# Rounding and subtracting a decoder step's weights 1024 columns at a time, in six tiles of their own

## The chip, the cores and the metric

The kernel runs on one core of one Trainium2 chip. The metric is the device time of one execution in microseconds (us). The core has five instruction streams that run side by side and wait for each other through semaphores: PE (matmuls, with their weight loads shown as PEld), ACT, DVE, POOL, and SP, which here issues all transfers between the chip's memory and the core's on-chip buffers.

## What is computed

One inference step of a one-layer hybrid decoder for 512 prompt tokens and 8 x 8 sample tokens, 576 columns in all, with a model width of 1024. Cut to what matters:

```python
mod = silu(c) @ w_ada + b_ada                 # six shifts and gains
u = x * (1 + sc1) + sh1
qa, ka, va, qh, fh, ih, ogh, gate_a, gate_b = split(u @ w_in)
attn = merge(dilated_attention(g) for g in ((128, 1), (512, 4), (2048, 16)))
hg = rms_norm(hgrn2(silu(qh), f, ih)) * silu(ogh)
merged = sigmoid(gate_a) * (attn @ w_branch_a) + sigmoid(gate_b) * (hg @ w_branch_b)
x1 = layer_norm(ALPHA * x + g1 * (merged @ w_out))
u2 = x1 * (1 + sc2) + sh2
x2 = layer_norm(ALPHA * x1 + g2 * (relu(u2 @ w_up + b_up) ** 2 @ w_down + b_down))
```

All arrays are fp32. Besides x2 the kernel returns the new key/value caches and the new HGRN2 states.

## The kernel before

**Products in three terms.** Every large product is made from rounded parts. A value w is split into `hi` (w rounded to the fp32r type, by an ACT copy) and `lo` (w minus hi, rounded, by a DVE subtraction). PE then adds three products: hi times hi, hi times lo and lo times hi. The activations are split the same way (`uh`/`ul`, `u2h`/`u2l`, `hdh`/`hdl` and so on).

**Weights.** `unit(...)` lists the weight blocks in the order of use. A unit is 8 (branch a: 4) k tiles of 128 rows by W columns, W being 256 or 512. `load_one` brings 8 KB a partition at a time into one of three `raw` buffers (`NRAW`), so a unit of 256 columns is one load, a unit of 512 columns two. A block of 128 columns is split by `split_slot`: for each four k tiles one ACT copy and one DVE subtraction of 4 x 128 = 512 columns, into two pages. Token units (`tok=True`: the v of the three attention groups and the two HGRN value units, with the tokens as the matmul's stationary operand) are split by `split_k`, one k tile of 512 columns at a time: four k tiles ahead of the first half of the unit, four ahead of the second (`split`, `j // 5 * 4`).

**Pages.** Nearly all tiles on the chip come from one pool, `pages`: `NPG` = 68 buffers of 2304 bytes a partition (576 fp32 columns). Activations, heads, scores, cache tiles (`kv`), broadcast queries (`qb`), states and the split weights share it. A tile gets a buffer when its first writer is put in order, and that writer waits until the last instruction that uses the buffer's former tile is done. Each engine runs its instructions strictly in the order in which the program lists them.

**The front and the back.** The front runs from the input to the branch products: all units up to `n_front`. Its first unit (`u0`, 512 columns, two loads) is special: three of its blocks (`n_early`) are split slot by slot and multiplied k tile by k tile (`early_mm`) as the input's k tiles `uh`/`ul` come into being (`make_u`), slot 0 before the first, slot 1 at the end of step s = 1. Then a loop goes over the blocks (`flat`): `ahead(i)` and `ahead(i + 1)` split the next block, `run_block` lists the matmuls of the current one and the evacuation of its result. The back (w_out, layer norm, the MLP's 32 up and 32 down blocks) follows after `side.drain()`.

**The order of the work.** Attention, the sample caches, HGRN and the ada products are generators in lanes of `Side`. After each group of up to 8 matmuls `side.pump` lets the lanes emit steps, by a planned clock of every engine (`Engine`: ACT 90 + 0.84 n, DVE 65 + 1.05 n, POOL 60 + 2.28 n ns for n columns). So the planned costs set where side steps fall among the matmuls.

Nearly every instruction is recorded through one helper, so the profile gives them all one line, L173; they are told apart by their tiles: `whi`/`wlo` the split weights, `wraw` a raw buffer, `lin` the result bank of the large products.

Of the kernel before, what the change touches and what calls it, by code (L numbers as in the profile page):

```python
# [12 lines left out]
F32R = mybir.dt.float32r  # L13
U8 = mybir.dt.uint8
AF = mybir.ActivationFunctionType
# [4 lines left out]
KT = D // 128  # L20
# [5 lines left out]
HF = NT // 2  # L26
# [22 lines left out]
LND = 1200  # L49
APART = 6  # L50
LNQ = 3200
NPG = 68
AHEAD_K = 8
LN2 = 2500
SPH = 0
NRAW = 3
# [187 lines left out]
def decoder_step(ctx, tc, I, O):  # L244
    nc = tc.nc
    consts = ctx.enter_context(tc.tile_pool(name="consts", bufs=1))
    pages = ctx.enter_context(tc.tile_pool(name="pages", bufs=NPG))
    raw = ctx.enter_context(tc.tile_pool(name="raw", bufs=NRAW))
    small = ctx.enter_context(tc.tile_pool(name="small", bufs=2))
    dram = ctx.enter_context(tc.tile_pool(name="dram", bufs=1, space=bass.MemoryType.DRAM))  # L250
    psum = ctx.enter_context(tc.tile_pool(name="psum", bufs=2, space=bass.MemoryType.PSUM))
# [2 lines left out]
    V, A = Engine(nc.vector, "DVE", 65.0, 1.05), Engine(nc.scalar, "ACT", 90.0, 0.84)  # L254
    G, PE, SP = Engine(nc.gpsimd, "POOL", 60.0, 2.28), Engine(nc.tensor, "PE", 0.0, 0.0), Engine(nc.sync, "SP", 0.0, 0.0)
# [5 lines left out]

    def page(shape, name, dtype=F32):
        return pages.tile(shape, dtype, name=name, tag="page")

    def bank(shape, tag, bufs=2):
        return psum.tile(shape, F32, name=tag, tag=tag, bufs=bufs)
# [30 lines left out]
    units = []  # L297

    def unit(src, row0, nk, col0, W, blocks, tok=False):
        units.append(dict(src=src, row0=row0, nk=nk, col0=col0, W=W, blocks=blocks, slots=[], w={}, tok=tok))  # L300
# [19 lines left out]
    def load_more(force=False):  # L320

        while leaving and (force or leaving[0] <= side.now):
            leaving.popleft()
        while load_q and live[0] + len(leaving) < NRAW:
            load_one()
# [3 lines left out]
    def loaded(u):  # L329
        return sum(kk for _, kk, _ in u["slots"]) == u["nk"]  # L330

    def weights_done(slots):
        live[0] -= len(slots)
        leaving.extend(Engine.read.get(t.tensor.name, 0.0) for _, _, t in slots)
        load_more()

    def split(u, j):


        def there():  # L340
            load_more(True)
            return len(u["slots"]) > j // 5 if u["tok"] else loaded(u)
        if not there():
            side.drain(("a", "s"), there)
        assert there()
        if u["tok"]:
            for k in range(j // 5 * 4, j // 5 * 4 + 4):
                split_k(u, k)
            return
        for s in range(len(u["slots"])):  # L350
            split_slot(u, j, s)
        if j == len(u["blocks"]) - 1:
            weights_done(u["slots"])

    def split_k(u, k, eng=V):

        if k in u["w"]:
            return
        load_more(True)
        t = u["slots"][k // 4][2][:, k % 4]  # L360
        w = u["w"][k] = page([128, 512], "whi", F32R), page([128, 512], "wlo", F32R)
        A.activation(w[0], t, AF.Copy)
        eng.tensor_sub(w[1], t, w[0])
        if k % 4 == 3:
            weights_done(u["slots"][k // 4:k // 4 + 1])

    def split_once(u, j):
# [1 line left out]
            u["split"].add(j)  # L369
            split(u, j)  # L370

    def split_slot(u, j, s):
        k0, kk, t = u["slots"][s]
        hi, lo = u["w"].setdefault(j, ([], []))
        for k in range(0, kk, 4):
            src = t[:, k:k + 4, j * 128:(j + 1) * 128]
            hi.append(page([128, 4, 128], "whi", F32R))
            lo.append(page([128, 4, 128], "wlo", F32R))
            A.activation(hi[-1], src, AF.Copy)
            V.tensor_sub(lo[-1], src, hi[-1])  # L380

    def mm_part(w, nk, xs, h, ps, ks):
        hi, lo = w
        seq = [(hi, 0), (hi, 1), (lo, 0)]
        n = 0
        for k in ks:
            for m, (ww, xi) in enumerate(seq):
                PE.matmul(ps, ww[k // 4][:, k % 4], xs[xi][k][:, h * HF:(h + 1) * HF],
                          start=(k == 0 and m == 0), stop=(k == nk - 1 and m == 2))
                n += 1  # L390
                if n % 8 == 0 and n < 3 * len(ks):
                    side.pump(8 * 123.0)
# [68 lines left out]
    def hv(t, h):  # L461
        return t[:, h * HF:(h + 1) * HF]
# [1028 lines left out]
    n_front = len(units)  # L1491
    for n0 in (0, 4):
        unit(I["w_out"][0], 0, 8, n0 * 128, 512, [None] * 4)
    for qd in range(4):
        for n0 in (0, 4):
            unit(I["w_up"][0], 0, 8, (qd * 8 + n0) * 128, 512, [None] * 4)
        for n0 in (0, 4) if qd < 3 else (4, 0, 4):
            unit(I["w_down"][0], qd * 1024, 8, n0 * 128, 512, [None] * 4, tok=(qd == 3))
    for u in units:
        for k0 in range(0, u["nk"], 2048 // u["W"]):  # L1500
            load_q.append((u, k0))
# [58 lines left out]
    xs = [page([128, 4, 128], "xs", F32R) for _ in range(2)]  # L1560
# [13 lines left out]
    u0 = units[0]  # L1574
# [9 lines left out]
    x_transposed(xa, range(4))  # L1584
    for j in range(n_early):
        done_split.add((id(u0), j))
        split_slot(u0, j, 0)
    shift = [ada(s, w) for s, w in enumerate(wa)]
    wa.clear()
    next(shift[0])  # L1590
    for s in range(4):
        next(shift[s])
        for k in (2 * s, 2 * s + 1):
            make_u(k)
        if s == 3:
            ahead(n_early)
        if s:
            early_mm(2 * s - 1)
        if s == 2:
            next(shift[3])  # L1600
        early_mm(2 * s)
        if s < 2:
            next(shift[s + 1])
            x_transposed(xb, (2 * s, 2 * s + 1))
        if s == 1:
            for j in range(n_early):
                split_slot(u0, j, 1)
    early_mm(KT - 1)
    shift.clear()
    for j in range(n_early):  # L1610
# [8 lines left out]
    for i, (u, j) in enumerate(flat):  # L1619
# [18 lines left out]
        if n_run == 20:  # L1638
            for e in range(2):
                t = page([128, 4, 128], "lmf")  # L1640
# [106 lines left out]
    for k in range(KT):  # L1747
        t = page([128, NT], "hT")
# [31 lines left out]
    def half(u, j, xs, h, evac):  # L1780
        ps = bank([128, HF], "lin")
        mm_half(u["w"][j], 8, xs, h, ps)
        evac(h, ps)
        side.pump(8 * 123.0)
# [4 lines left out]
    u = mlp[0]  # L1789
# [75 lines left out]
    ud = mlp[14:17]  # L1865
    for i, (u, j, xs, ev) in enumerate(seq):
        if i < 4:
            for k in (2 * i, 2 * i + 1):
                for h in range(2):
                    G.tensor_mul(hv(hT[k], h), hv(hT[k], h), rstds[h])  # L1870
        if i == n_down:
            side.add("p", residual())
        if i + 1 < len(seq):
            split(*seq[i + 1][:2])
        else:
            for k in range(AHEAD_K):
                split_k(ud[0], k)
        if i >= 8:
            copy_rows()
        for h in range(2):  # L1880
            half(u, j, xs, h, ev)
        u["w"].pop(j)
# [85 lines left out]
    def blocks(w, e):  # L1968
        for n in range(4):
            ps = bank([128, NT - NM], "lin")  # L1970
            for k in range(KT):
                if n == 0 and k + AHEAD_K < KT:
                    split_k(w, k + AHEAD_K)
                for m, (xi, wi) in enumerate(TERMS):
                    PE.matmul(ps, w["w"][k][wi][:, n * 128:(n + 1) * 128], HD[xi][k][:, NM:NT],
                              start=(k == 0 and m == 0), stop=(k == KT - 1 and m == 2))
                if n == 3 and w is ud[0]:
                    pass_on(w, k, ud[1])
                if k % 2 and k < KT - 1:
                    side.pump(6 * 136.0)  # L1980
            gated(hT[4 * e + n], ps, slice(NM, NT), 5, 4 * e + n)
            side.add("pr"[n % 2], tokens_major(4 * e + n))
            side.pump(6 * 136.0)

    def pass_on(u, k, v):

        if k >= 2:
            u["w"].pop(k - 2)
        if k >= KT - AHEAD_K:
            split_k(v, k - KT + AHEAD_K)  # L1990

    def tiles(w, e):
        for c in range(NM // 128):
            last = c == NM // 128 - 1

            def before(k):
                if w is ud[1]:
                    if last and k >= 2:
                        w["w"].pop(k - 2)
                    if k % 2 == SPH:  # L2000
                        split_k(ud[2], 4 * c + k // 2, V if c else G)

            for cols in (slice(0, 256), slice(256, 512)) if e and last else (slice(0, 512),):
                ps = mm_tokens(w["w"], HD, lambda t: t[:, c * 128:c * 128 + 128], range(KT), before, cols,
                               "att" if cols.start else "lin")
                add_up(c, e, ps, cols)
            if e:
                if last:
                    side.drain()
                moments(c, c + 1)  # L2010
                normalize(c, last)
# [43 lines left out]
```

## Time and profile before

| | us |
|---|---|
| median of 3 runs | 1381.82 |
| lowest and highest of the 3 | 1379.16 and 1386.65 |
| the profiled execution | 1381.52 |
| its span in the profile | 1379.7 |

The mean granted clock of the profiled execution was 0.989. Its busy times and the rows behind them are shown where the prediction uses them. In a row of a group, "xN | a, b | c" is the number of instructions, their busy time in us, the mean of one in ns, and the engine's idle time in us just before them with what ended it. In a row of the timeline the first two numbers are the start and the time in us, and the bracket holds the idle time before it with what ended that. In a row of waits stand the us in total, the number of waits and the longest.

### The profile page before, as it was taken

To read this page: it belongs to the slowest core of one execution; us is meant where nothing else is said; L and a number is where in the kernel's file an instruction comes from. 1 tells how busy PE (TensorE), PEld (TensorE's weight loads), DVE (VectorE), ACT (ScalarE), POOL (GpSimd) and SP (SyncE) were. 2 spreads that over 40 slices of the span, in tenths; PEclk is the share of its full clock that TensorE was granted. 3 is DMA by queue.
4 is the path that set the end of the run, shared out by engine and by line. 5 is a ranking of instruction groups with operands and counts; after the bars stand their busy time and mean duration, and the time that the engine had idled before them with its cause. 6 is when DMAs were issued, how large, how long until landed. Compare 5 with 4: busy or idle time off the path is not lost.

```text
span 1379.7 us, 24690 instructions
## 1 busy us (share of the span) xinstructions
PE 1330.6 (96%) x9624; PEld 1228.2 (89%) x9624; DVE 766.6 (56%) x1572; ACT 469.5 (34%) x1101; POOL 359.9 (26%) x419
## 2 busy tenths in 40 slices
PE   6999999999899999999999999999999999999995
PEld 3899898799778887888899999998999999999994
DVE  2456555558767886566655446547522333354458
ACT  3423333332422232333233441325554422413522
POOL 1242023026417563234344200003500200200205
PEclk9999999999999999999999999999999999999998
DMA  9789899689989977776445223331123633522322
GB/s 295 255 306 341 268 317 339 238 272 324 280 282 285 319 243 242 240 239 199 147 157 170 70 73 112 130 123 62 62 107 129 237 124 147 220 77 91 118 99 69
DMA packets 184520, 269.40 MB, mean 195 GB/s; under 512 B 15756, under 2 KB 92372, under 8 KB 183892
## 3 DMA queue, kind: packets, MB, share of 16 engines
q1 hardware_dynamic: 184404, 267.83, 57.7%
q8 instruction: 76, 1.25, 0.4%
q14 instruction: 40, 0.33, 0.1%
HBM read 210.45 MB, written 74.10 MB: 206 GB/s over the span
## 4 chain that ended last, share of the span: by engine, by line
PE 83%; DVE 6%; DMA 4%; ACT 2%; issue 2%; POOL 2%; SPq 1%; DVEq 0%; POOLq 0%; ACTq 0%
PE lin L173 68%; PE att L173 7%; PE tr L173 4%; PE sx L173 4%; DVE wlo L173 2%; DMA out_dram<-kv 2%; DVE res L173 1%; DMA kv<-in_cache_kv_w_dram 1%; POOL qb L173 1%; ACT whi L173 1%; SPq L173 1%; DMA xtm<-in_x_prompt_dram 0%; DMA wraw<-in_w_ada_dram 0%; DMA qb<-qsc 0%; DVE st L173 0%
## 5 line engine op out<-in xcount | busy, mean ns | idle before, releaser
L173 DVE TENSOR_TENSOR wlo<-wraw,whi 128x512 fp32r<-128x512 f32 x340 | 248.4, 774 | 128.5 <-ACT whi L173 125.7
L173 PE MATMUL lin<-uh,whi 128*128 128x288 f32 x992 | 298.4, 301 | 4.3 <-DVE hso L173 2.4
L173 PE MATMUL lin<-uh,wlo 128*128 128x288 f32 x992 | 298.2, 301 | 2.3 <-DVE wlo L173 2.3
L173 PE MATMUL lin<-ul,whi 128*128 128x288 f32 x992 | 299.3, 302 | 1.0 <-DVE ul L173 0.9
L173 ACT ACTIVATE whi<-wraw 128x512 fp32r<-128x512 f32 x344 | 193.4, 620 | 112.8 <-DMA wraw<-in_w_down_dram 29.7
L173 PEld LDWEIGHTS lin<-ul,whi 128*128 128x128 f32 x992 | 187.6, 189 | 13.7 <-issue 10.9
L173 PEld LDWEIGHTS lin<-uh,whi 128*128 128x128 f32 x992 | 187.5, 189 | 10.3 <-DVE hso L173 2.7
L173 PEld LDWEIGHTS lin<-uh,wlo 128*128 128x128 f32 x992 | 187.7, 189 | 7.1 <-issue 3.8
L173 POOL TENSOR_TENSOR qb<-qb,kv 128x512 f32<-128x512 f32 x96 | 128.3, 1356 | 204.0 <-DMA qb<-qsc 90.7
L173 PE MATMUL lin<-u2h,whi 128*128 128x288 f32 x496 | 147.1, 297 | 1.2 <-ACT u2h L173 1.2
L173 PE MATMUL lin<-u2l,whi 128*128 128x288 f32 x496 | 147.0, 296 | 0.3 <-DVE u2l L173 0.3
L173 PE MATMUL lin<-u2h,wlo 128*128 128x288 f32 x496 | 146.8, 296 | 0.0
L173 PE MATMUL lin<-hdh,whi 128*128 128x288 f32 (+1 forms) x448 | 133.6, 298 | 0.2 <-ACT hdh L173 0.2
L173 PE MATMUL lin<-hdl,whi 128*128 128x288 f32 (+1 forms) x448 | 132.9, 297 | 0.1
L173 PE MATMUL lin<-hdh,wlo 128*128 128x288 f32 (+1 forms) x448 | 133.0, 297 | 0.0
L173 POOL TENSOR_TENSOR rel<-rel 128x288 f32<-128x288 f32 x56 | 38.3, 684 | 292.7 <-ACT rel L173 287.7
L173 PEld LDWEIGHTS lin<-u2h,whi 128*128 128x128 f32 x496 | 93.4, 188 | 1.8 <-ACT u2h L173 1.5
L173 PEld LDWEIGHTS lin<-u2l,whi 128*128 128x128 f32 x496 | 93.3, 188 | 1.5 <-DVE u2l L173 0.9
L173 DVE TENSOR_TENSOR hdl<-rel,hdh 128x288 fp32r<-128x288 f32 x61 | 28.4, 466 | 118.5 <-ACT hdh L173 118.5
L173 PEld LDWEIGHTS lin<-u2h,wlo 128*128 128x128 f32 x496 | 93.3, 188 | 0.5 <-issue 0.5
L173 PEld LDWEIGHTS lin<-hdh,whi 128*128 128x128 f32 x448 | 84.1, 188 | 0.7 <-ACT hdh L173 0.4
L173 PEld LDWEIGHTS lin<-hdl,whi 128*128 128x128 f32 x448 | 84.1, 188 | 0.3 <-DVE hdl L173 0.3
(358 smaller groups left out, 2546.6 us busy)
## 6 DMA issues: line engine op xcount, KB each, us to landing
wraw<-in_w_in_dram SPq DMA_DIRECT2D x42, 1024.0 KB
kv<-in_cache_kv_w_dram SPq DMA_DIRECT2D x144, 256.0 KB
qb<-qsc SPq DMA_DIRECT2D x96, 256.0 KB
wraw<-in_w_down_dram SPq DMA_DIRECT2D x18, 1024.0 KB
out_dram<-kv SPq DMA_DIRECT2D x64, 256.0 KB
wraw<-in_w_ada_dram SPq DMA_DIRECT2D x16, 1024.0 KB
wraw<-in_w_up_dram SPq DMA_DIRECT2D x16, 1024.0 KB
out_dram<-in_cache_kv_w_dram SPq DMA_DIRECT2D x32, 512.0 KB
```

The costliest lines, as they stand in the source:

```text
L173: return f(out, *args, **kw)
```

## The change

The front's splits become twice as wide where a raw buffer holds enough, and they move from the pages into a pool of their own: `NWP` = 6 tiles of 8 x 128 fp32 columns (4 KB a partition). The pages are 59 instead of 68, so that 9 x 2304 = 20736 bytes a partition go and 24576 come.

- A block of a 256-column unit is split by one ACT copy and one DVE subtraction of 8 x 128 columns. Blocks of the first unit and of branch a keep 512 columns (a raw buffer holds four of their k tiles) but use the new tiles as well.
- A token unit's k tiles go in pairs of 2 x 512 columns for k = 0 to 5; k = 6 and 7 are split one by one into pages as before.
- The back is split as before (`four`, `two=False`), into pages.
- `AHEAD_K` goes: it was 8, the number of k tiles, so nothing changes by that.

```diff
-NPG = 68
-AHEAD_K = 8
+NPG = 59
+NWP = 6
...
+    parts = ctx.enter_context(tc.tile_pool(name="parts", bufs=NWP))
...
+    def wpart(shape, name, dtype=F32R):
+
+        return parts.tile(shape, dtype, name=name, tag="part")
...
         if u["tok"]:
             for k in range(j // 5 * 4, j // 5 * 4 + 4):
-                split_k(u, k)
+                split_k(u, k, two=(k < 6))
             return
-        for s in range(len(u["slots"])):
-            split_slot(u, j, s)
+        split_block(u, j, four=u.get("four", False))
...
+        k -= k % 2
+        t = u["slots"][k // 4][2][:, k % 4:k % 4 + 2]
+        hi, lo = wpart([128, 2, 512], "whi"), wpart([128, 2, 512], "wlo")
+        A.activation(hi, t, AF.Copy)
+        eng.tensor_sub(lo, t, hi)
+        for i in range(2):
+            u["w"][k + i] = hi[:, i], lo[:, i]
+        if k % 4 == 2:
             weights_done(u["slots"][k // 4:k // 4 + 1])
...
-    def split_slot(u, j, s):
-        k0, kk, t = u["slots"][s]
-        hi, lo = u["w"].setdefault(j, ([], []))
-        for k in range(0, kk, 4):
-            src = t[:, k:k + 4, j * 128:(j + 1) * 128]
-            hi.append(page([128, 4, 128], "whi", F32R))
-            lo.append(page([128, 4, 128], "wlo", F32R))
-            A.activation(hi[-1], src, AF.Copy)
-            V.tensor_sub(lo[-1], src, hi[-1])
+    def split_block(u, j, slots=None, four=False):
+
+        if j not in u["w"]:
+            u["w"][j] = [], []
+        for k0, kk, t in u["slots"] if slots is None else [u["slots"][s] for s in slots]:
+            if four:
+                for k in range(0, kk, 4):
+                    split_rows(u, j, t[:, k:k + 4, j * 128:(j + 1) * 128], page)
+            else:
+                split_rows(u, j, t[:, :, j * 128:(j + 1) * 128], wpart)
+
+    def split_rows(u, j, src, home):
+        hi, lo = (home(list(src.shape), nm, F32R) for nm in ("whi", "wlo"))
+        A.activation(hi, src, AF.Copy)
+        V.tensor_sub(lo, src, hi)
+        for k in range(src.shape[1]):
+            for part, t in zip(u["w"][j], (hi, lo)):
+                part.append(t[:, k])
...
+    for u in units[n_front:]:
+        u["four"] = True
...
     for j in range(n_early):
         done_split.add((id(u0), j))
-        split_slot(u0, j, 0)
+        split_block(u0, j, (0,))
...
         if s == 1:
             for j in range(n_early):
-                split_slot(u0, j, 1)
+                split_block(u0, j, (1,))
```

More of the change, by code (lines that the diff above doesn't have):

```diff
@@ L347, in split, with split_k @@
             for k in range(j // 5 * 4, j // 5 * 4 + 4):
-                split_k(u, k)
+                split_k(u, k, two=(k < 6))
             return
-        for s in range(len(u["slots"])):
-            split_slot(u, j, s)
+        split_block(u, j, four=u.get("four", False))
         if j == len(u["blocks"]) - 1:
             weights_done(u["slots"])
-    def split_k(u, k, eng=V):
+    def split_k(u, k, eng=V, two=True):
         if k in u["w"]:
@@ L359, in split_k @@
         load_more(True)
[L360 to L364, printed above, removed]
+        if not two:
+            t = u["slots"][k // 4][2][:, k % 4]
+            w = u["w"][k] = page([128, 512], "whi", F32R), page([128, 512], "wlo", F32R)
+            A.activation(w[0], t, AF.Copy)
+            eng.tensor_sub(w[1], t, w[0])
+            if k % 4 == 3:
+                weights_done(u["slots"][k // 4:k // 4 + 1])
+            return
+        k -= k % 2
[6 more added lines that the diff above has]
+        if k % 4 == 2:
             weights_done(u["slots"][k // 4:k // 4 + 1])
@@ L387, in mm_part @@
             for m, (ww, xi) in enumerate(seq):
-                PE.matmul(ps, ww[k // 4][:, k % 4], xs[xi][k][:, h * HF:(h + 1) * HF],
+                PE.matmul(ps, ww[k], xs[xi][k][:, h * HF:(h + 1) * HF],
                           start=(k == 0 and m == 0), stop=(k == nk - 1 and m == 2))
@@ L1875, in decoder_step @@
         else:
-            for k in range(AHEAD_K):
-                split_k(ud[0], k)
+            for k in range(KT):
+                split_k(ud[0], k, two=False)
         if i >= 8:
@@ L1971, in blocks @@
             for k in range(KT):
-                if n == 0 and k + AHEAD_K < KT:
-                    split_k(w, k + AHEAD_K)
                 for m, (xi, wi) in enumerate(TERMS):
@@ L1988, in pass_on @@
             u["w"].pop(k - 2)
-        if k >= KT - AHEAD_K:
-            split_k(v, k - KT + AHEAD_K)
+        split_k(v, k, two=False)
     def tiles(w, e):
@@ L2000, in before @@
                     if k % 2 == SPH:
-                        split_k(ud[2], 4 * c + k // 2, V if c else G)
+                        split_k(ud[2], 4 * c + k // 2, V if c else G, False)
             for cols in (slice(0, 256), slice(256, 512)) if e and last else (slice(0, 512),):
```

## The prediction

> **What bounds the kernel now.** I read the page first (busy times, chain), then busy times by stage, then the front's weight splits, then who made PE's weight loads wait in the front. "Split" below is the rounding of a weight piece (ACT writes `whi`) and the subtraction (DVE writes `wlo`).
>
> ```profile
> span 1379.7 us, 24690 instructions
> PE 1330.6 (96%) x9624; PEld 1228.2 (89%) x9624; DVE 766.6 (56%) x1572; ACT 469.5 (34%) x1101; POOL 359.9 (26%) x419
> ...
> PE 83%; DVE 6%; DMA 4%; ACT 2%; issue 2%; POOL 2%; SPq 1%; DVEq 0%; POOLq 0%; ACTq 0%
> ```
>
> ```profile
> 60.00:430.00 370.00, 360.49 (x2414) 326.56 (x2413) 227.06 (x452) 113.49 (x302) 105.59 (x85) 0.99 0.88 294
> 430.00:620.00 190.00, 181.38 (x1335) 155.01 (x1336) 138.36 (x271) 58.29 (x152) 92.06 (x100) 0.98 0.81 263
> 620.00:830.00 210.00, 209.13 (x1670) 192.01 (x1670) 114.43 (x273) 73.25 (x182) 64.05 (x82) 1.00 0.44 137
> 975.00:1300.00 325.00, 325.00 (x2460) 325.00 (x2459) 119.88 (x224) 126.00 (x255) 47.96 (x65) 1.00 0.35 130
> ```
>
> Columns: stretch, length, busy PE, PEld, DVE, ACT, POOL, granted clock, DMA share, GB/s. PE sets the end: 83% of the chain, and from 975 to 1300 us it never pauses. DVE holds 6% of the chain; it is busiest between 60 and 620 us (227.06 + 138.36 = 365 of 560 us). The change merges instructions on ACT and DVE and leaves PE's count alone, so it can only win back what PE loses by waiting for those two in the front.
>
> ```profile
> L173 DVE TENSOR_TENSOR wlo<-wraw,whi x167: 675/686/4556, 59.8 to 827.7; 128x512 fp32r<-128x512 f32 x167
> L173 ACT ACTIVATE whi<-wraw x171: 612/622/637, 59.7 to 826.1; 128x512 fp32r<-128x512 f32 x171
> ```
>
> ```profile
> PEld lin L173 <- DVE wlo L173: 6.7, 6, 2.5
> PEld att L173 <- DVE S L173: 3.4, 1, 3.4
> PEld lin L173 <- DVE hso L173: 2.7, 1, 2.7
> PEld att L173 <- DVE qp L173: 2.1, 1, 2.1
> PEld lin L173 <- ACT whi L173: 1.8, 2, 1.6
> PEld tr L173 <- DVE Op L173: 1.7, 1, 1.7
> ```
>
> First fence: min/median/max in ns between 60 and 830 us. Second: us in total, times, longest. Of 167 subtractions, six keep PE waiting, 6.7 us in all, and two roundings 1.8 us: nearly every split is done before PE wants it. With S, hso, qp and Op, PE's waits for DVE come to 6.7 + 3.4 + 2.7 + 2.1 + 1.7 = 16.6 us. That is the stake.
>
> **The change part by part.** *Instructions.* By the code the front has 192 splits: 34 units of eight k tiles with two blocks of two pieces (136), 8 for the first unit, 8 for branch a, 5 token units of 8. Afterwards: 68, 8, 8 and 5 x 5 (three pairs, two singles) = 109. So 83 instructions go from ACT and 83 from DVE. The price of a wider one comes from two widths of the same kind of work, that of a pair from a run of four:
>
> ```profile
> L173 ACT ACTIVATE hdh<-rel 128x288 fp32r<-128x288 f32 x64 | 28.5, 445 | 51.0 <-POOL rel L173 50.8
> L173 DVE TENSOR_TENSOR hdl<-rel,hdh 128x288 fp32r<-128x288 f32 x61 | 28.4, 466 | 118.5 <-ACT hdh L173 118.5
> L173 DVE TENSOR_TENSOR hgl<-hg,hgh 128x576 fp32r<-128x576 f32 x8 | 6.0, 752 | 0.0
> L173 ACT ACTIVATE hgh<-hg 128x576 fp32r<-128x576 f32 x8 | 5.4, 674 | 0.0
> ```
>
> ```profile
> 307.35 2.18 ACT L173 ACTIVATE whi<-wraw 128x512 fp32r<-128x512 f32 x4
> ```
>
> ```profile
> 59.84 2.50 DVE L173 TENSOR_TENSOR wlo<-wraw,whi 128x512 fp32r<-128x512 f32 x4 [3.42 <-ACT whi L173]
> ```
>
> DVE: (752 - 466)/288 = 0.99 ns a column, so 1024 columns take 686 + 508 = 1194 ns. Two of 512 take 1372 ns apart, but in a queue each further one adds only (2.50 - 0.69)/3 = 0.60 us, a pair 1.29. A merge saves 0.10 to 0.18 us: 8 to 15 us over 83. ACT: 0.80 ns a column, 1024 take 622 + 407 = 1029 ns; a pair in a queue 0.62 + 0.52 = 1.14 us; 0.11 to 0.21 us a merge, 9 to 18 us. I take the low ends, since the splits stand in queues. ACT's gain lies beside PE (ACT is busy 113 of 370 us) and I cost it at nothing; if that cover failed, the two whi waits of 1.8 us are all it could win.
>
> [...]
>
> *DVE behind POOL.* The larger effect may be the hold-ups:
>
> ```profile
> 498.78 6.22 DVE L173 TENSOR_TENSOR wlo<-wraw,whi 128x512 fp32r<-128x512 f32 x2
> ```
>
> ```profile
> 496.54 7.92 POOL L173 TENSOR_TENSOR qb<-qb,kv 128x512 f32<-128x512 f32 x6
> ```
>
> ```profile
> 506.03 0.49 PE L173 MATMUL att<-S,hq 128*128 128x128 f32 x2 [3.17 <-DVE S L173]
> ```
>
> ```profile
> L173 DVE TENSOR_TENSOR wlo<-wraw,whi 128x512 fp32r<-128x512 f32 x167 | 130.8, 827 | 79.0 <-ACT whi L173 78.1 <-DMA kv<-in_cache_kv_w_dram 0.7
> ```
>
> Two subtractions take 6.22 us instead of 1.29 while POOL runs six multiplies without a gap, and PE then stands 3.17 us for the S that was queued behind them. Over the front the mean is 827 against a median of 686 ns: 167 x 0.141 = 23.5 us of such hold-ups. If they are met once per instruction, losing 83 of 192 saves 43% of them, 10 us; if they last as long as POOL's run does, nothing. Together DVE is relieved of 8 to 25 us of its 365. PE's share lies between 0 and the 16.6 + 1.8 us it waits; I take a third of 16.6, **5.5 us off**, nearer the low end, since a wait ends where the next late input begins (ACT sb or POOL hk in the same places).
>
> *Start, added.* The first unit splits two slots for three blocks: 12 tiles out of six. So the three roundings of slot 1 must wait until the early matmuls of k=3 have read slot 0:
>
> ```profile
> 43.05 1.66 ACT L173 ACTIVATE whi<-wraw 128x512 fp32r<-128x512 f32 x3
> 46.14 0.82 ACT L173 ACTIVATE uh<-xT,mod 128x512 fp32r<-128x512 f32 x1 [1.42 <-issue]
> ```
>
> ```profile
> 43.71 1.90 DVE L173 TENSOR_TENSOR wlo<-wraw,whi 128x512 fp32r<-128x512 f32 x3 [0.72 <-ACT whi L173]
> 45.52 0.30 DVE L173 TENSOR_REDUCE mt<-tr 128x36 f32<-128x144 f32 x1
> ```
>
> ```profile
> 45.79 0.29 PE L173 MATMUL sx<-uh,wlo 128*128 128x288 f32 x1
> 46.01 1.92 PE L173 MATMUL tr<-wada,cT 128*32 128x512 f32 x16
> 48.31 0.40 PE L173 MATMUL lin<-ul,whi 128*128 128x288 f32 x1
> ```
>
> k=3 ends at 46.1. The third rounding then runs to 46.7, its subtraction to 47.4, and `mt`, queued behind it on DVE, starts there instead of at 45.52; behind `mt` come `mod` and the u of k=4, on ACT the uh of k=4 and 5, and PE waits for exactly these at 48.31. **+1.8 us**, nothing to hide it (0 if slot 1 lands late anyway, 2.4 with a rounding more). Later waits for a part are covered: a block's two, or a token half's four, reuse parts that PE left a block earlier, and ACT reaches them behind that block's evacuation.
>
> *Latency, added.* PE's first matmul of a block now waits for 1024 columns: `whi` 1.03 instead of 0.62 us, `wlo` 1.03 + 1.19 = 2.22 instead of 0.62 + 0.69 = 1.31 us after the start, +0.9 us where nothing was ahead, +0.5 where DVE's queue was late (1.19 against 0.69). PE waited for a split eight times, so 0 to 8 x 0.9 = 7.2 us. I take **+2 us**: most of the eight end with a held-up subtraction, where the pair's end counts.
>
> *Pages, moved.* Blocks in flight held 8 of 68 pages, so 60 were left; now 59, and 55 while a token unit keeps k=6 and 7 in four pages. In the back U2, hT, acc and Hd take 48, two blocks 8, rel 2: 58 of 59, cost 0, hidden by ACT's spare time (126 of 325 us busy), at most one rounding (0.6 us) a block if it were gone. SP's order of loads and stores stays, since a slot is given back behind its last split as before. The planner charges fewer instructions and may move side steps by a group of matmuls; no row prices that, and I leave it at nothing, inside the range.
>
> Sum: 1381.5 (the profiled execution; span 1379.7 plus 1.8 around it) - 5.5 + 1.8 + 2.0 = 1379.8, say **1380.0 us**. The median of three runs is 1381.82, practically the same base.
>
> **The rivals.** *Hidden anyway:* splits are ahead in all but eight places, and DVE's relief ends in idle time; the added parts remain: 1381.5 + 1.8 + 0 to 2 = 1383 to 1385. For it: PE's 16.6 us sit in few places with different causes.
>
> *Hold-ups vanish:* each subtraction meets POOL once, pairs met it twice, and the long waits go: 12 to 16 of the 16.6 us, start cost paid: 1367 to 1372. For it: the 6.22 us pair; against it: POOL's runs stay as long. [...]
>
> *Pages run short (slower):* the pool already runs out once:
>
> ```profile
> 505.70 0.41 ACT L173 ACTIVATE hf<-lin 128x288 f32<-128x288 f32 x1 [6.88 <-DVE sc L173]
> ...
> 543.70 2.19 ACT L173 ACTIVATE whi<-wraw 128x512 fp32r<-128x512 f32 x4
> ```
>
> ACT stands 6.88 us before an evacuation until DVE has read a qb: only that buffer's page can be what it needs. From 430 to 620 us the HGRN heads and the cache tiles fill the pool. The token unit whose second half is split at 543.70 then has 55 pages. It decides once the other tiles need more than that; ACT's evacuations, and SP's kv, S0 and qb loads with weight loads and stores behind them, would wait. In that stretch PE stood 3.17 us; two or three such stretches more cost 6 to 10 us, with 1.8 + 2: 1391 to 1395.
>
> **How the numbers follow.** About 0.5% of 1381.8, 6.9 us, is what a measurement of this kernel can tell from no change: faster is below 1374.9, slower above 1388.7. Forecast 0.40 and hidden 0.20, both within: 0.60. Hold-ups vanish: 0.22, faster. Pages short: 0.18, slower. The range 1369 to 1391 takes in most of the faster rival and the near end of the slower one and leaves out about 0.18. The likeliest case's own range is 1376 to 1385.
>
> **What would show it.** `whi` falls from 344 to 261; its wide form takes about 1.03 us, the wide `wlo` 1.2 (more is hold-up). DVE busy between 60 and 620 us falls from 365 to about 350. The uh of k=4 starts near 48 instead of 46.1. PE's waits for DVE fall to about 11 us. Wrong would be: waits for wlo longer than 6.7 us (latency), the same sum with DVE relieved (hidden), or evacuations and SP held for a page between 430 and 620 us.

## The result, and the profile after

The changed kernel takes 1392.05 us (median of five runs, 1389.22 to 1393.40); the kernel before, beside it, 1382.62 us. The ratio is 1.0064, 95% interval [1.0040, 1.0088]. It is slower by about 9 us, 1 us above the predicted range and inside the 1391 to 1395 us of the rival "pages run short". A second set of runs of the same kernel gave 1391.92 us, ratio 1.0047 [1.0033, 1.0061]. The profiled execution took 1390.6 us.

The page of the kernel after (span, busy times, chain):

```profile
span 1388.8 us, 24549 instructions
...
PE 1332.2 (96%) x9624; PEld 1226.8 (88%) x9624; DVE 755.2 (54%) x1489; ACT 463.5 (33%) x1018; POOL 364.9 (26%) x419
...
PE 74%; DVE 6%; issue 4%; DMA 3%; ACT 2%; POOL 1%; SPq 0%; DVEq 0%; POOLq 0%; ACTq 0%
```

DVE lost 83 instructions and 11.4 us of work, ACT 83 and 6.0 us; PE's busy time is the same within 1.6 us. The span is 9.1 us longer, so the loss is waiting. The groups by shape between 60 and 840 us (busy us, mean ns of one, then the idle time before them and what ended it):

```profile
L173 DVE TENSOR_TENSOR wlo<-wraw,whi 128x1024 fp32r<-128x1024 f32 x75 | 107.5, 1438 | 85.4 <-ACT whi L173 69.5 <-DMA qb<-qsc 13.0 <-DMA out_dram<-kv 2.2
...
L173 ACT ACTIVATE whi<-wraw 128x1024 fp32r<-128x1024 f32 x76 | 79.0, 1053 | 40.1 <-PE lin L173 20.4 <-DMA wraw<-in_w_in_dram 19.6
```

The wide rounding costs what was forecast (1053 ns against 1029). The wide subtraction has a mean of 1438 ns, 244 above the forecast of 1194; before, two narrow ones had 2 x 141 = 282 ns of hold-up. The two kernels run in different orders, so this pair of numbers does not yet tell what the width does; the narrow kernel below does. What PE's weight loads waited for, 60 to 840 us (total, times, longest):

```profile
PEld lin L173 <- DVE wlo L173: 11.8, 11, 5.1
...
PEld sx L173 <- ACT moda L173: 5.1, 2, 4.2
...
PEld lin L173 <- DVE hq L173: 2.0, 1, 2.0
PEld sx L173 <- ACT KT L173: 1.9, 2, 1.4
PEld lin L173 <- DVE hvs L173: 1.8, 1, 1.8
PEld lin L173 <- DVE vtm L173: 1.7, 2, 0.8
...
PEld att L173 <- ACT hktm L173: 1.0, 1, 1.0
```

The wait for `wlo` did not fall; it went from 6.7 to 11.8 us. The waits for ACT's `moda` and `KT`, and that of `att` for `hktm`, are new in the list. The long one for `moda` comes with the changed order of the work: it is 4.3 us in the kernel before in the new order with 70 pages, one of the experiments below. Busy time by stage, with the bounds moved along with the work:

```profile
60.00:435.00 375.00, 364.09 (x2455) 328.14 (x2455) 229.37 (x418) 113.27 (x274) 116.07 (x91) 1.00 0.90 297
435.00:626.00 191.00, 177.05 (x1294) 151.46 (x1295) 123.35 (x240) 53.57 (x132) 81.67 (x88) 0.96 0.75 245
...
985.00:1310.00 325.00, 325.00 (x2459) 325.00 (x2458) 119.45 (x225) 127.27 (x254) 48.02 (x65) 1.00 0.35 131
```

Between 435 and 626 us PE is idle for 13.95 of 191 us; before it was 8.62 of 190. The bounds do not fall at the same matmul, but from 60 to 620 us before and from 60 to 626 us after stand the same 3748 matmuls: PE is idle for 18.1 us before and 24.9 us after. In the back PE is busy 325.00 of 325.00 us as before. DVE between 60 and 626 us has 229.37 + 123.35 = 353 us instead of 365: relieved as forecast, and PE got nothing of it.

### The profile page after: what moved, and what is told of

Its sections match the earlier page's. It is cut to its first block, busy times and chain, and to the rows that moved or that the text cites. A ratio compares the mean times of both kernels' runs of the same rounds, so it can differ in the third digit from the quotient of the medians.

```text
span 1388.8 us, 24549 instructions
## 1 busy us (share of the span) xinstructions
PE 1332.2 (96%) x9624; PEld 1226.8 (88%) x9624; DVE 755.2 (54%) x1489; ACT 463.5 (33%) x1018; POOL 364.9 (26%) x419
## 4 chain that ended last, share of the span: by engine, by line
PE 74%; DVE 6%; issue 4%; DMA 3%; ACT 2%; POOL 1%; SPq 0%; DVEq 0%; POOLq 0%; ACTq 0%
PE lin L173 63%; PE att L173 6%; PE tr L173 3%; PE sx L173 3%; DVE wlo L173 2%; DMA out_dram<-kv 1%; DMA qb<-qsc 1%; DVE res L173 1%; ACT whi L173 1%; DMA wraw<-in_w_in_dram 1%; POOL qb L173 1%; SPq L173 0%; DMA out_dram<-S 0%; DVE sc L173 0%; DVE hq L173 0%
## 5 line engine op out<-in xcount | busy, mean ns | idle before, releaser
L173 DVE TENSOR_TENSOR wlo<-wraw,whi 128x512 fp32r<-128x512 f32 (+1 forms) x257 | 239.3, 960 | 154.0 <-ACT whi L173 136.2
L173 ACT ACTIVATE whi<-wraw 128x512 fp32r<-128x512 f32 (+1 forms) x261 | 187.9, 758 | 142.2 <-PE lin L173 65.7
L173 POOL TENSOR_TENSOR qb<-qb,kv 128x512 f32<-128x512 f32 x96 | 135.9, 1433 | 203.1 <-DMA kv<-in_cache_kv_w_dram 84.2
```

What stands on the lines that cost most here:

```text
L173: return f(out, *args, **kw)
```

## The experiments

Twelve kernels in four sets on three chips, each set beside the kernel before on its own chip (medians of before 1382.66 to 1383.76 us), five rounds each. "Order" means the order in which the planner emits the instructions of an engine. The charges for fewer splits had changed it: with the splits left out and the rest compared place by place by the names of the tiles, PE's list differs between the traces of before and after in 2580 of 9624 places, DVE's in 446 of 1232, SP's in 206 of 771, ACT's in 161 of 757, POOL's in 54 of 419.

| kernel | order | median us | ratio to before, 95% interval |
|---|---|---|---|
| before, 64 pages | old | 1403.07 | 1.0146 [1.0118, 1.0174] |
| before, 70 pages | old | 1383.55 | 0.9993 [0.9979, 1.0007] |
| before in the new order, 67 pages | new | 1381.64 | 0.9982 [0.9965, 0.9999] |
| before in the new order, 68 pages | new | 1379.70 | 0.9976 [0.9958, 0.9993] |
| before in the new order, 70 pages | new | 1379.45 | 0.9962 [0.9947, 0.9976] |
| the same with 68 pages, caches copied from DRAM | new | 1380.73 | 0.9983 [0.9966, 0.9999] |
| after, again | new | 1391.92 | 1.0047 [1.0033, 1.0061] |
| after, first unit in pages | new | 1389.93 | 1.0048 [1.0030, 1.0067] |
| after, narrow | new | 1388.62 | 1.0039 [1.0023, 1.0055] |
| after, narrow and first unit in pages | new | 1390.22 | 1.0039 [1.0027, 1.0050] |
| after, caches copied from DRAM | new | 1385.59 | 1.0011 [0.9992, 1.0030] |
| after, all three | new | 1382.56 | 1.0002 [0.9987, 1.0016] |

Kernels of the new order run the same PE instructions in the same sequence, so their traces can be laid side by side matmul by matmul. The table gives the start of the n-th matmul that reads a split weight (`whi` or `wlo`). The first column is the kernel before in the new order with 70 pages, the others say how much later it starts there (us, worked out from the traces; "end" is the last matmul):

```
  n   70 pages |  after  again  first  narrow  narrow+  DRAM  all three | 68 pages
                                in pg          first    copies
   0     23.0  |   +0.9   +0.6   +0.2   +0.4    +0.2    +0.3    +0.7    |   +0.8
 300     91.4  |   +5.8   +5.6   +2.1   +4.7    +2.7    +4.5    +3.8    |   +2.8
1500    324.0  |   +6.4   +6.3   +1.9   +4.7    +2.2    +5.2    +4.0    |   +2.6
2400    529.6  |   +5.8   +7.6   +3.5   +1.5    +4.4    +1.1    +6.1    |   +3.8
2700    613.4  |  +12.5  +14.1   +9.9   +8.0   +12.2    +3.0    +7.7    |   +4.5
 end   1366.7  |  +12.9  +14.6  +11.0   +7.8   +11.8    +4.4    +8.3    |   +5.5
```

One step stands out: 84 us of work, from 529.6 to 613.4 us, in which every kernel with 59 pages loses 6.4 to 7.8 us, except the two whose caches are copied from DRAM (1.9 and 1.6); with 67 pages it is 2.0, with 68 it is 0.7. Each column is one execution, up to 4 us from its kernel's median (all three: 1386.35 profiled, median 1382.56), so single entries scatter by some us; the step is alike in all five kernels that have it.

**The order alone.** The kernel before, with its 68 pages and narrow splits, but the planner charged as in the kernel after:

```diff
+    def planned(eng, outs, ins, n):
+        end = eng.enter(outs, ins, eng.fixed + eng.rate * n, 60.0)
+        Engine.top = max(Engine.top, end)
...
+            planned(A, [x[0] for x in w], [t], 1024)
+            planned(V, [x[1] for x in w], [t] + [x[0] for x in w], 1024)
+            for i in range(2):
+                nc.scalar.activation(w[i][0], t[:, i], AF.Copy)
+                nc.vector.tensor_sub(w[i][1], t[:, i], w[i][0])
```

> The kernel before with its 68 pages and its 512-column splits, but the planner charges the front's splits as the changed kernel does, so that every engine gets its other instructions in the changed kernel's order. Planner theory: as slow as the changed kernel less its start, 1387 to 1391. Pages theory and width theory: like the kernel before, 1381 to 1385.

It is faster than before by 3.1 us (1379.70 against 1382.78 beside it), which neither theory expected, and its sisters with 67 and 70 pages and with copied caches have ratios of 0.9962 to 0.9983, all below 1. With 70 pages it is the fastest kernel here, ahead of both. So the tiles, pages and widths of the change cost about 12 us, of which the order gives 3 back. Which wait the order saves was not tried, so this gain has no cause shown.

**Fewer pages, more pages.**

```diff
-NPG = 68
+NPG = 64
```

> The kernel before with 64 pages instead of 68, nothing else changed. Pages theory: the pool already runs out with 68 between 430 and 600 us, so four pages fewer cost 4 to 10 us, 1387 to 1393, with new waits of SP, ACT and POOL for a page in that stretch. Planner and width theory: no change, 1381 to 1384.

Four pages fewer cost 20 us, twice the most that was expected, and the place is the same: its matmuls are 2.35 us later than before at 535 us and 19.45 at 619, and no more after that. The other direction, NPG = 70 in the old and in the new order:

> The kernel before, in its own order, with 70 pages instead of 68. Theory (pages bind at 68): 1 to 5 us faster, 1377.5 to 1381.5 us, and ScalarE's wait of 6.88 us ahead of an evacuation at 505 us shrinks or goes. Rival (68 just enough): 1382.5 us, and that wait costs nothing.

> The kernel before in the order of the kernel after, with 70 pages instead of 68. Four pages fewer cost the kernel before 20 us between 535 and 619 us. Theory (pages still bind at 68, at the places where ScalarE stands for a page whose reader or store has not finished): two more give 1 to 5 us back there, 1375 to 1379. Rival (68 pages are just enough, the price rises steeply below only): 1379.7 us as with 68.

Both rivals hold: two more pages give nothing in either order (ratio 0.9993 [0.9979, 1.0007] in the old one; 1379.45 us against 1379.70 with 68 pages in the new one). ACT's timeline of the kernel before with 70 pages:

```profile
504.63 0.41 ACT L173 ACTIVATE hf<-lin 128x288 f32<-128x288 f32 x1 [1.55 <-POOL qb L173]
```

The wait ahead of this evacuation, 6.88 us with 68 pages, was for a page, as the slower rival had it, since two pages more cut it to 1.55 us; but it cost PE nothing (its wait for `S` behind it is 3.18 us with 70 pages, 3.17 with 68). And one page fewer, NPG = 67 in the new order:

> The kernel before in the new order with 67 pages, one fewer. Theory (the number of pages left for the side work decides; 59 beside the six tiles are 60 beside eight split pages less one, 67 less eight): a loss of 3 to 7 us appears between 533 and 620 us, 1382.5 to 1387 us. Rival (the fixed division decides, a ring of pages that the splits may share is enough at 67 too): 1379 to 1381 us.

By its time the rival holds again: 1381.64 us, ratio 0.9982 [0.9965, 0.9999], not to be told from 68 pages. Its trace shows that the shortage begins all the same: against 70 pages it loses nothing up to 567 us and 2.1 us by 590, in two waits of PE that the kernel with 70 pages does not have (PE's timeline with 67 pages):

```profile
582.10 0.66 PE L173 MATMUL sx<-ident,moda 128*128 128x128 f32 x4 [0.75 <-ACT moda L173]
588.44 0.33 PE L173 MATMUL sx<-ident,sb 128*128 128x128 f32 x1 [1.02 <-ACT sb L173]
```

The kernel after has these two waits in the same lengths, and others ahead of them. By the prediction's count (pages less eight for the blocks in flight) 67 leave 59, as many as the kernel after has, but they cost a third of what the kernel after loses in this stretch (2.0 of 6.7 us).

**The start.** The first unit's splits of the kernel after go to pages again:

```diff
-        split_block(u0, j, (0,))
+        split_block(u0, j, (0,), four=True)
...
-                split_block(u0, j, (1,))
+                split_block(u0, j, (1,), four=True)
```

> The changed kernel with the first unit's splits put into pages, 512 columns each, as before; all else as changed. The changed kernel lags the one before by 1.5 us at the early matmuls of k=4 and 0.4 us more at the fourth block, both behind slot 1 of that unit. If the six tiles are the cause of that lag and it reaches the end, the time is about 2 us under the changed kernel's 1392.1: 1390. If later waits swallow it (pages short theory), it stays within 1 us of 1392. In the trace the third rounding of slot 1 should start near 43 us again instead of 46.8.

1389.93 us, 2.0 to 2.1 less than the kernel after, but the intervals overlap, and the ratio of 1.0048 is that of the second set of the kernel after (1.0047). The place itself is clear: in the kernel after PE stands 0.86 us for the `uh` of k=4 (at 49.54 us) and 0.65 for its `ul`, in this one it waits for neither. The lags agree: at 91 us the four kernels whose first unit uses the six tiles are 4.5 to 5.8 us late (mean 5.2), the three of the same pools that use pages 2.1 to 3.8 (mean 2.9): 2.3 us, with kernels of 70, 67 and 68 pages at 0, 0.3 and 2.8 as a measure of the scatter.

**The width.** Every wide split of the kernel after as two half-width ones, into the same wide tiles, charged to the planner as before:

```diff
-        A.activation(hi, t, AF.Copy)
-        eng.tensor_sub(lo, t, hi)
+        planned(A, hi, [t], 1024)
+        planned(eng, lo, [t, hi], 1024)
         for i in range(2):
+            nc.scalar.activation(hi[:, i], t[:, i], AF.Copy)
+            nc.vector.tensor_sub(lo[:, i], t[:, i], hi[:, i])
```

> The changed kernel with the same tiles, pages and planned order, but each wide split done by two ACT and two DVE instructions of half the width. Pages theory (the loss comes from fewer pages) and planner theory (from the changed order of side work): within 2 us of the changed kernel, 1390 to 1394. Width theory (PE waits longer for the first columns of a wide split): the lag of 0.9, 0.4 and 0.65 us at the token units' second halves goes, 1389 or less. If the width is worth what the prediction took for it (5.5 us of PE's waits for DVE), it is slower than the changed kernel, 1395 to 1398.

1388.62 us: the 83 instructions come back and the kernel is, if anything, 3.4 us faster. Both edits together, and the kernel after once more beside them:

> The kernel after with both earlier edits at once: the first unit's splits in pages, and every wide split as two half-width roundings and two half-width subtractions; six tiles of 4 KB and 59 pages stay, the order of the other instructions is that of the kernel after. Theory (three separate costs: about 2.1 us at the start, 3.4 us for the width, and the rest from the six tiles taken out of the pool of pages): the two savings add, 1392.0 - 2.1 - 3.4 = 1386.5 us, and the lag behind the kernel before in the new order is still about 5.8 us between 533 and 600 us. Rival (the two edits save one and the same wait): 1388 to 1390. Rival (no cost of the pages is left once start and width are undone): near the 1379.7 us of the kernel before in the new order.

> The kernel after, unchanged, beside the other three on the same chip, so that the differences of a few us between them do not rest on two chips. If the earlier differences are the kernels' own: 1392 us, 5 to 6 us above the narrow one with its first unit in pages. If the chips differ by that much: another distance.

1390.22 us, not 1386.5, and the kernel after on the same chip is 1.7 us above it (1391.92), not 5 to 6: in the times the two savings don't add, and with the first unit in pages narrow and wide are alike (1390.22 and 1389.93). So what the width costs lies between 0 and 3.4 us and isn't settled by these runs; that it gains nothing is shown.

It does relieve DVE. In the same tiles and the same order DVE is busy for 768.3 and 772.6 us in the two narrow kernels, and for 755.2, 755.4 and 752.5 us in the three wide ones. The narrow kernel's subtractions of whole blocks, 60 to 840 us (busy us and mean ns; then min/median/max in ns):

```profile
L410 DVE TENSOR_TENSOR wlo<-wraw,whi 128x512 fp32r<-128x512 f32 x132 | 113.3, 895 | 59.9 <-ACT whi L409 57.9 <-DMA out_dram<-kv 1.7
```

```profile
L410 DVE TENSOR_TENSOR wlo<-wraw,whi x132: 660/685/8834, 59.3 to 839.2; 128x512 fp32r<-128x512 f32 x132
```

A narrow subtraction is held up by 895 - 685 = 210 ns on average, a wide one by 1438 - 1225 = 213 (in the other traces 257 narrow, 226 and 253 wide): in these traces hold-ups are met once per instruction, and fewer instructions meet fewer of them. That they come with POOL's work is worked out from the traces of before and after. Of the 340 narrow subtractions of the kernel before, the 262 that no POOL instruction runs beside take at most 0.69 us, the other 78 a mean of 1.07 and up to 4.56; of the 83 wide ones of the kernel after, 51 take at most 1.24 us, the other 32, beside POOL, a mean of 1.73 and up to 8.94. Why PE gets nothing of it is seen at one place that all these kernels have. The timelines of DVE, POOL and PE of the kernel after:

```profile
441.42 8.94 DVE L173 TENSOR_TENSOR wlo<-wraw,whi 128x1024 fp32r<-128x1024 f32 x1 [0.70 <-ACT whi L173]
```

```profile
441.86 9.64 POOL L173 TENSOR_TENSOR qb<-qb,kv 128x512 f32<-128x512 f32 x7
```

```profile
450.41 0.61 PE L173 MATMUL lin<-uh,wlo 128*128 128x288 f32 x1 [4.82 <-DVE wlo L173]
```

and of the narrow kernel with its first unit in pages:

```profile
437.20 10.68 DVE L410 TENSOR_TENSOR wlo<-wraw,whi 128x512 fp32r<-128x512 f32 x2 [0.27 <-ACT whi L409]
```

```profile
438.07 8.66 POOL L173 TENSOR_TENSOR qb<-qb,kv 128x512 f32<-128x512 f32 x7
```

```profile
447.33 0.61 PE L173 MATMUL lin<-uh,wlo 128*128 128x288 f32 x1 [5.54 <-DVE wlo L410]
```

(L410 and L409 are the same splits, recorded at lines of their own.) Of the two narrow subtractions the first takes 10.08 us, and the second follows at once in its usual 0.68: one held instruction before, one held instruction after, and PE stands 4.8 or 5.5 us either way. The wait belongs to POOL's run, though not to the end of it. In the kernel after DVE is done 1.1 us before the run of seven is, and it seems to get in at the seventh multiply, which takes 2.26 us instead of the usual 1.26 (POOL's timeline):

```profile
449.23 2.26 POOL L173 TENSOR_TENSOR qb<-qb,kv 128x512 f32<-128x512 f32 x1
```

In the narrow kernel it waits for all seven, in the kernel after with copied caches for three (5.30 us, PE's wait 1.18). What decides this the runs do not show.

**The pages of the cache stage.** In the kernel after, the loss between 529.6 and 613.4 us begins with two evacuations on ACT (its timeline), of `hktm` (a transposed tile of HGRN) and `KT` (a transposed cache tile). PE waits for what they write, and for `moda` and `sb` behind them (PE's timeline):

```profile
563.42 0.60 ACT L173 ACTIVATE hktm<-tr 128x512 f32<-128x512 f32 x1 [17.83 <-DMA out_dram<-kv]
...
585.25 0.60 ACT L173 ACTIVATE KT<-sx 128x512 f32<-128x512 f32 x1 [4.51 <-DMA out_dram<-S]
```

```profile
564.07 1.16 PE L173 MATMUL att<-hvtm,hktm 128*128 128x128 f32 x8 [0.60 <-ACT hktm L173]
...
585.90 1.92 PE L173 MATMUL sx<-wraw,cT 128*32 128x512 f32 x16 [1.16 <-ACT KT L173]
...
592.04 0.66 PE L173 MATMUL sx<-ident,moda 128*128 128x128 f32 x4 [0.75 <-ACT moda L173]
...
598.38 0.33 PE L173 MATMUL sx<-ident,sb 128*128 128x128 f32 x1 [1.02 <-ACT sb L173]
```

What ended ACT's waits is not its input but a store out of an old `kv` page and one out of an old state page `S`: the new tile was given that page. In the kernel before in the new order with 70 pages the first wait ends with its input (its waits):

```profile
ACT hktm L173 <- PE tr L173: 13.9, 1, 13.9
```

The experiment frees the `kv` pages earlier. The old cache rows go to the new cache from the input in DRAM, at the same place of SP's queue, so a `kv` page is free once PE has read it:

```diff
-        SP.dma_start(kv_rows(g, x, r, out_s[g][0, b], True), kv.pop((g, b, r, x))[skip:128])
+        t = kv.pop((g, b, r, x))
+        src = kv_rows(g, x, r, cache_in[g][0, b], False)
+        SP.dma_start(kv_rows(g, x, r, out_s[g][0, b], True), src[skip:128] if g < 2 else src)
```

> The kernel after, but the copies of the old cache rows into the new caches are read from the input in DRAM instead of from the kv page; the same stores stand at the same places of SyncE's queue, and a kv page is free as soon as TensorE has read it, not when its store has landed. The order of all engines is the same. Theory (pages run short in the cache stage: 6.5 us are lost between 533 and 626 us, from ScalarE's wait of 17.8 us for a page whose store has to land): that wait goes, the lag behind the kernel before in the new order grows by less than 2 us there, 1385 to 1388 us. Rival (another tile's page is late next, or the caches' being read twice delays the weights, DMA share 0.8 in this stretch): 1391 us or more.

> The kernel before in the new order (68 pages), with the same edit as the run on the kernel after: old cache rows copied from DRAM. Theory (68 pages are enough, 70 gave nothing): earlier release gives nothing, 1379 to 1381 us; so what the edit gives the kernel after is the pages' price. Rival (reading the caches twice costs): above 1382 us, and the same cost is then to be added to the run on the kernel after.

The kernel after gains 6.3 to 6.5 us by the medians (1385.59 us, the interval [0.9992, 1.0030] lies below both of the kernel after); as the chips differ, the distance to the kernel before beside each says the same, 1.8 us instead of 8.9 and 9.4. The kernel before in the new order gains nothing (1380.73 against 1379.70). ACT's timeline of the kernel after with copied caches:

```profile
557.26 0.60 ACT L173 ACTIVATE hktm<-tr 128x512 f32<-128x512 f32 x1 [16.29 <-PE sx L173]
...
577.24 0.60 ACT L173 ACTIVATE KT<-sx 128x512 f32<-128x512 f32 x1 [2.65 <-PE sx L173]
```

No store ends these waits any more. `KT` waits for PE's `sx`, its input. `hktm`, whose input is `tr`, still waits for a page, but now only until PE has read the old `kv` tile (its `sx<-kv,pt` begins at 556.18 us and takes 1.07), which is what the edit was to do. The same 628 PE instructions, by the windows of three kernels (length, then PE busy): 70 pages in the new order, after, and after with copied caches:

```profile
529.60:613.40 83.80, 83.80 (x628) 69.98 (x627) 54.96 (x127) 27.40 (x72) 25.15 (x36) 1.00 0.64 212
```

```profile
535.35:625.85 90.50, 85.42 (x628) 70.00 (x627) 53.21 (x120) 26.61 (x65) 24.98 (x36) 1.00 0.61 195
```

```profile
530.75:616.40 85.65, 84.51 (x628) 70.02 (x627) 53.91 (x120) 26.59 (x65) 25.50 (x36) 1.00 0.64 207
```

PE idles 5.08 us in the kernel after, not at all with 70 pages, 1.14 us with copied caches: 3.9 us of idle time go, and 4.85 us of the stretch's length. The rest of the 6.3 to 6.5 us lies outside this stretch. In that one trace PE's wait behind POOL is 1.18 us instead of 4.82; whether the copies do that, or chance, is not shown. DMA is no busier in the kernel that is slow (share 0.61 against 0.64), so it isn't load that holds the pages back.

**All three undone** (first unit in pages, narrow, copied caches):

> The kernel after with all three edits at once: the first unit's splits in pages, every wide split as two half-width instructions on each engine, the old cache rows copied from DRAM; six tiles of 4 KB, 59 pages and the order stay. Theory (start, width and the pages of the cache stage are all that the kernel after loses to the kernel before in the new order): 1380 to 1382 us, as the kernel before in the new order with the same copies (1380.7). Rival (start and width cost nothing measurable; the pages of the cache stage are the only price there, and some 4 us more are lost elsewhere to the smaller pool): 1384 to 1386 us, as without those two edits.

1382.56 us, between the two expectations: 1.8 us above the kernel before in the new order with the same copies, and 3.0 below the one with copies alone. Neither distance is outside the intervals.

## Why the prediction was wrong

- **Pages, moved: the step that failed.** The prediction counted "now 59, and 55 while a token unit keeps k=6 and 7", showed that the back needs 58, and put cost 0 into the sum; the front it did not count, and left to a rival with 0.18. The back was right (PE 325.00 of 325.00 us). In the front the six fixed tiles cost 4.9 us between 535 and 626 us by the traces (3.9 of them idle time of PE), and 6.3 to 6.5 us by the medians, in the stretch that the rival named and in its way: ACT's evacuations stand for a page, PE behind them. Copied caches take that back; start and width do not change it (the step is there in all three variants without the copies). The count itself was also the wrong measure: 67 shared pages leave 59 by it and lose 2.0 us there in the trace, where the kernel after loses 6.7, and nothing that their times show. That six tiles set apart can't be lent to the side work when no split is in flight would explain this; it was argued from the code, not tried.
- **A third of 16.6 us, 5.5 us off: wrong, at the step from DVE's relief to PE's wait.** DVE was relieved by 12 us between 60 and 626 us, as forecast (8 to 25), and by 13 to 20 us beside the narrow kernels of the same order. The hold-ups shrank as in the first of the prediction's two models, "once per instruction". But PE's five largest waits for DVE went from 16.6 to 11.8 + 2.0 + 1.8 + 1.7 + 1.4 (`sc`) = 18.7 us instead of to 11. The largest of them stands behind one run of POOL's, where one held instruction stays one held instruction, so for PE the other model held: "if they last as long as POOL's run does, nothing". In the kernel after the multiply at which DVE seems to get in took 2.26 us instead of 1.26. DVE was passed over for six multiplies in a row there and for seven in the narrow kernel, and at this place fewer subtractions did not wait less: 8.94 us for the wide one, 10.08 and 0.68 for the two narrow ones.
- **Start, +1.8 us: about right.** The three roundings of slot 1 wait for slot 0, DVE's `mt` behind them (ACT's and DVE's timelines of the kernel after):

```profile
45.18 0.63 ACT L173 ACTIVATE whi<-wraw 128x512 fp32r<-128x512 f32 x1 [1.28 <-PE lin L173]
45.98 0.63 ACT L173 ACTIVATE whi<-wraw 128x512 fp32r<-128x512 f32 x1 [0.17 <-PE att L173]
46.78 0.63 ACT L173 ACTIVATE whi<-wraw 128x512 fp32r<-128x512 f32 x1 [0.17 <-PE sx L173]
48.67 0.81 ACT L173 ACTIVATE uh<-xT,mod 128x512 fp32r<-128x512 f32 x1 [1.26 <-DVE mod L173]
```

```profile
45.84 2.30 DVE L173 TENSOR_TENSOR wlo<-wraw,whi 128x512 fp32r<-128x512 f32 x3 [2.12 <-ACT whi L173]
48.05 0.30 DVE L173 TENSOR_REDUCE mt<-tr 128x36 f32<-128x144 f32 x1
```

`mt` starts at 48.05 instead of 45.52, the `uh` at 48.67 instead of 46.14: 2.5 us, of which the first matmul's own delay against before is 0.8. That leaves 1.7; PE's two waits there are 1.5 us, the comparison of traces gives 2.3, and the times 2.0 to 2.1 with overlapping intervals.
- **Latency, +2 us: the right sign, size open.** The wait for `wlo` rose from 6.7 to 11.8 us. What PE's weight loads waited for in the narrow kernel with its first unit in the six tiles, 60 to 840 us:

```profile
PEld lin L173 <- DVE wlo L410: 4.9, 2, 4.5
...
PEld lin L173 <- DVE wlo L383: 1.8, 2, 0.9
```

With 0.9 us more for the single splits of k=6 and 7 that is 7.6 us. But 4 to 5 us of each total are one wait behind POOL near 447 us, whose length changes from kernel to kernel (1.2 to 6.1 us in the four wide ones, 4.3 to 5.5 in the three narrow ones with 59 pages), and the times say 0 to 3.4 us for the width.
- **The planner, "left at nothing": wrong by 3 us,** in the change's favour. No row of before prices an order; only the run in the new order does.

The sum with what was measured, on the kernel before in the new order (1379.7): start 2, pages 5 to 6.4, and some 4 to 5 us that width, latency and the smaller pool elsewhere share and that no run separates: 1392. On record stood 1381.5 - 5.5 + 1.8 + 2 + 0 + 0. The start was near, two terms were put at nothing (the pages of the front, the planner's order), and the only gain did not come.

## What to carry to other kernels

Buffers taken out of a shared pool for a private use are a cost of their own (here 4.9 us by the traces, 6.3 to 6.5 by the medians): count the demand in the fullest stage, not only in the one you know best, and read which store or reader ends the waits ahead of evacuations there. Do not book an engine's relief as time unless the wait that PE sees gets shorter: DVE's hold-ups shrank with the number of its instructions, but the one that PE waited for did not, since it lasted as long as POOL's run kept DVE out (PE stood 4.82 us behind one wide subtraction, 5.54 behind two narrow ones). Where a planner sets the order by charges, run the old work in the new order first; here that alone was 3 us, and the best kernel.

## What the runs showed of the hardware

- DVE's subtraction of two tiles stood behind six and seven of POOL's multiplies in a row: 8.94 us for one of 1024 columns behind six of them in the kernel after (median 1225 ns of the 95 splits of the front, 75 of them wide), 10.08 us for one of 512 columns behind seven in the narrow kernel with its first unit in pages. At the end of the wait in the kernel after one of POOL's multiplies took 2.26 us, the six before it 1.26 to 1.29. Summed over the front the hold-up went by the number of instructions, not by their width: 210 ns on average at 512 columns (narrow kernel), 213 at 1024 (kernel after).
- Reading 144 cache tiles of 240 to 256 KB a second time, from DRAM to DRAM instead of from the core's memory, cost nothing that can be measured (1380.73 against 1379.70 us, ratios 0.9983 [0.9966, 0.9999] and 0.9976 [0.9958, 0.9993]), with a DMA share of 0.65 from 532 to 617 us. In the kernel after the share from 430 to 620 us is 0.79 with these copies, 0.77 without.
- The price of pages was not in proportion to their number: by the times 70 and 68 are alike in the old order, 70, 68 and 67 in the new one, and 64 cost 20 us in the old. Traces show the onset sooner: 67 pages lose 2.0 us in the cache stage against 70, which the times do not show.
